# Down-block sums and left-operand sums on GpSimd, operand blocks in two steps, and a last product in two column halves

## The chip, the cores and the metric

The kernel runs on one core of a Trainium2 chip. The metric is device microseconds of one execution, the median of several runs. The engines are TensorE (PE in the profile; PEld is its weight load), VectorE (DVE), ScalarE (ACT), GpSimd (POOL) and SyncE (SP), which here issues the transfers.

## The reference

One encoder layer is applied to two groups of rows that share the weights: 1024 new frames and 32 frames of a running stream. The kernel keeps them side by side as 1056 columns of one activation `x` (1024 features in 8 tiles of 128 partitions). Cut to what matters here:

```python
x = x + 0.5 * swiglu(rms_norm(x, ffn1_norm), ffn1_w_gate, ffn1_w_up, ffn1_w_down)
...   # conv group, HGRN2 group, output projection, attention over 256 memory tokens
x = x + 0.5 * swiglu(rms_norm(x, ffn2_norm), ffn2_w_gate, ffn2_w_up, ffn2_w_down)
y = rms_norm(x, final_norm)      # rms over the 1024 features of a frame

def swiglu(x, w_gate, w_up, w_down):            # 1024 -> 2816 -> 1024
    return (jax.nn.silu(x @ w_gate) * (x @ w_up)) @ w_down
```

Everything is float32. The change touches the two feed-forward networks (FFN1, FFN2) and the final norm.

## The kernel before

**Products.** Each float32 operand is split into a high half (rounded to the type `fp32r`, made by ScalarE) and a low half (operand minus high half, made by VectorE). A product takes three passes on TensorE: high by high, weight high by activation low, weight low by activation high. So a block of weights is usable once ScalarE and then VectorE have worked on it (`Blocks.block`, L498 and L499, for the up products; `DownBlocks.make`, L588 and L589, for the down products).

**Seven products for eight.** Most of each FFN goes by a scheme of Strassen's kind: operands are cut in 2 x 2 quarters, and sums of quarters are multiplied, in the order `a11, s2, s3, a12, s1, a22, s4` for up and `a11, s1, s2, s3, a22, s4, a12` for down (`DORDER`). The sums of the activations ("left operands") for the up products are made in place in `x` by `build` (L784 through its `add`, 16 for each FFN), after the normed rows were made; the sums of the up weights by `Blocks.make` (L513). In the down phase the sums of weights are made by `DownBlocks.make`, one for each of 6 blocks of four of the seven kinds (L576 s1, L579 s2, L582 s3, L584 a22), and the sums of the hidden activations were made in the up phase and lie in memory, from where `Hidden.load` (L543) brings them and `Hidden.split` splits them (L296, L297).

**Down phase.** `down_phase` runs over 7 kinds, 4 row tiles `mp` of 128 output features and 11 k steps. A k step is six matmuls of 264 columns (L876, L877, L880, two column halves `u` each), 48 of them to a block of 8 k steps. At the first k step of a block it asks for the third block after it (`blocks.ready(b + 3)`). After the 11 k steps `take` adds the product to the residual `x` (L828, and L839/L842 for a running sum `u`), whose halves `load_x` (L824) brings back from memory during the first three kinds. Raw weights come in 512 KB tiles (`wraw`, 4 buffers; high and low halves have 3 buffers each).

**What sets the order.** The FFNs are written under a manual schedule: on the engines of `START` (VectorE, TensorE, ScalarE) instructions run in the order in which the code writes them. Generators are interleaved with the products: `tick()` after each k step advances background jobs, each by its rate (`bg(job, 1.0)` is one yield a tick), and `ready(n)` advances a block generator until n blocks are made. One yield of `Blocks`, `DownBlocks` or `build` is one block or one sum.

**End of the program.** In FFN2's down phase `last2` is called for each finished half row tile of `x`: ScalarE squares it, VectorE adds the squares to `r_t`, and ScalarE scales it by the final norm's gain (L1834). When the second column half is complete, `first_tokens` (0.2 yields a tick) turns and writes token tiles 5 to 8. For the first half, `last_tokens` runs for each pair of row tiles, `(4,5)`, `(6,7)`, `(0,1)`, `(2,3)`: it waits five yields, then turns the columns of token tiles 0 to 4 with transposes on TensorE into `pxf` and `pxs` (L1887), and ScalarE copies them to `y`. The last pair comes with no wait and after the last matmul: sums over features by matmuls with a column of ones (`col_norm`, L1850), a reciprocal root in ten small steps on VectorE (`col_root` L334, `rsqrt`), scaling of `y` in three parts (L1895, L1896, L1897) and five transfers (L1898).

## Time and profile before

| | |
|---|---|
| time, median of 3 runs | 2235.58 us (2233.88 to 2236.37) |
| profiled execution, its own time | 2238.53 us |
| its span | 2236.8 us |
| TensorE busy | 2188.3 us, 98% |
| VectorE busy | 1534.8 us, 69% |
| ScalarE busy | 854.2 us, 38% |
| GpSimd busy | 3.5 us, 20 instructions |
| transfers | 262.56 MB, mean 117 GB/s |

The profile is of one execution. A row of the groups reads: engine, tile written and tiles read, count, then busy time and mean length of one, then the idle time of the engine just ahead of them and who ended it. A row of single instructions begins with its start and length in microseconds; what stands in square brackets at its end is the engine's idle time ahead of it and who ended it. A window row gives, for each engine, busy time and count of instructions, then the granted TensorE clock as a share of full speed, the transfer engines' busy share and GB/s.

### The profile page before, as it was taken

The page shows a single profiled execution, that of the slowest core. Times are in us where ns is not written, and L with a number is a line of the kernel's source. Part 1 is how long each engine was busy: PE and PEld are TensorE (multiplying, and loading weights), DVE is VectorE, ACT ScalarE, POOL GpSimd, SP SyncE. Part 2 cuts the span into 40 slices and gives each one's busy share as a digit, 9 for nine tenths or more (in the row PEclk, how much of TensorE's full clock was granted, in tenths as well). Part 3 has the DMA queues.
Part 4 walks back from the last instruction along what each step waited for, and adds up shares of the span by engine and source line. Part 5 has one row for each costly group of instructions (what it writes and reads, how often), then busy time and mean ns, then how long its engine had stood idle before and what let it go on. Part 6 is the DMA issues. An engine that isn't in the chain of part 4 may idle for free. (4 is left out here: it accounts for less than half of the span.)

```text
span 2236.8 us, 39733 instructions
## 1 busy us (share of the span) xinstructions
PE 2188.3 (98%) x16381; PEld 2136.8 (96%) x16381; DVE 1534.8 (69%) x2502; ACT 854.2 (38%) x1550; POOL 3.5 (0%) x20
## 2 busy tenths in 40 slices
PE   8999999999999999999999999999999999999996
PEld 7999999999999899999889999999999999999896
DVE  6976666676777868898643665588866666667763
ACT  6342322333345512455651432352422322343353
POOL 0000000000000000000000000000000000000000
PEclk9999999999999999999999999999999999999998
DMA  6233233249876721111121211121333233298661
GB/s 212 73 110 125 78 98 116 84 136 310 244 225 185 225 79 50 30 42 38 35 95 54 62 52 53 43 107 48 106 99 116 84 97 119 75 297 256 194 181 64
DMA packets 312407, 262.56 MB, mean 117 GB/s; under 512 B 12580, under 2 KB 251912, under 8 KB 312226
## 3 DMA queue, kind: packets, MB, share of 16 engines
q1 hardware_dynamic: 312226, 260.02, 37.6%
q8 instruction: 129, 2.11, 0.4%
q14 instruction: 52, 0.43, 0.1%
HBM read 196.20 MB, written 63.77 MB: 116 GB/s over the span
## 5 line engine op out<-in xcount | busy, mean ns | idle before, releaser
L690 PE MATMUL ps<-A,vhi 128*128 128x264 f32 x1216 | 321.0, 284 | 2.1 <-DVE t L749 2.1
L691 PE MATMUL ps<-A,vhi 128*128 128x264 f32 x1216 | 320.6, 284 | 0.0
L694 PE MATMUL ps<-A,vlo 128*128 128x264 f32 x1216 | 247.4, 285 | 0.0
L691 PE MATMUL pa<-a,vhi 128*128 128x264 f32 x912 | 241.6, 285 | 0.0
L690 PE MATMUL pa<-a,vhi 128*128 128x264 f32 x912 | 241.4, 285 | 0.0
L876 PE MATMUL pdn<-A,vhi 128*128 128x264 f32 x880 | 234.5, 287 | 4.7 <-ACT vhi L588 4.7
L877 PE MATMUL pdn<-A,vhi 128*128 128x264 f32 x880 | 233.2, 286 | 0.0
L690 PEld LDWEIGHTS ps<-A,vhi 128*128 128x128 f32 x1216 | 229.1, 188 | 2.5 <-DVE t L749 2.3
L691 PEld LDWEIGHTS ps<-A,vhi 128*128 128x128 f32 x1216 | 228.7, 188 | 0.0
L694 PEld LDWEIGHTS ps<-A,vlo 128*128 128x128 f32 x1216 | 188.3, 188 | 0.0
L694 PE MATMUL pa<-a,vlo 128*128 128x264 f32 x912 | 185.0, 284 | 0.0
L880 PE MATMUL pdn<-A,vlo 128*128 128x264 f32 x880 | 181.1, 287 | 1.6 <-DVE vlo L589 1.5
L876 PEld LDWEIGHTS pdn<-A,vhi 128*128 128x128 f32 x880 | 167.4, 190 | 5.5 <-ACT vhi L588 5.5
L690 PEld LDWEIGHTS pa<-a,vhi 128*128 128x128 f32 x912 | 171.9, 189 | 0.0
L206 ACT ACTIVATE whi<-wraw 128x1024 fp32r<-128x1024 f32 x74 | 78.1, 1058 | 245.5 <-PE pwo L215 51.3
L691 PEld LDWEIGHTS pa<-a,vhi 128*128 128x128 f32 x912 | 171.3, 188 | 0.0
L877 PEld LDWEIGHTS pdn<-A,vhi 128*128 128x128 f32 x880 | 166.8, 190 | 0.0
L1224 DVE SCALAR_TENSOR_TENSOR ycv<-uy,dwc,ycv 128x1086 f32<-128x1086 f32 x120 | 157.0, 1342 | 0.6
L694 PEld LDWEIGHTS pa<-a,vlo 128*128 128x128 f32 x912 | 141.3, 188 | 0.0
L499 DVE TENSOR_TENSOR vlo<-b_s,vhi 128x512 fp32r<-128x512 f32 x114 | 78.7, 691 | 91.0 <-ACT vhi L498 91.0
L880 PEld LDWEIGHTS pdn<-A,vlo 128*128 128x128 f32 x880 | 137.5, 190 | 3.4 <-DVE vlo L589 3.2
L498 ACT ACTIVATE vhi<-b_s 128x512 fp32r<-128x512 f32 x114 | 71.2, 625 | 175.8 <-DVE b_s L513 174.8
(385 smaller groups left out, 5302.8 us busy)
## 6 DMA issues: line engine op xcount, KB each, us to landing
hd<-t SPq DMA_DIRECT2D x154, 264.0 KB
hraw<-hd SPq DMA_DIRECT2D x154, 264.0 KB
wraw<-in_ffn_w_up SPq DMA_DIRECT2D x44, 512.0 KB
wraw<-in_ffn_w_gate SPq DMA_DIRECT2D x42, 512.0 KB
wraw<-in_ffn_w_down SPq DMA_DIRECT2D x36, 512.0 KB
wraw<-in_w_in SPq DMA_DIRECT2D x24, 512.0 KB
xd<-x SPq DMA_DIRECT2D x32, 264.0 KB
x<-xd SPq DMA_DIRECT2D x32, 264.0 KB
```

Of the source, the lines that this page charges most:

```text
L206: act.activation(hi, t[:, :w], AF.Copy)
L498: act.activation(hi, src, AF.Copy)
L499: dve.tensor_tensor(lo, src, f32(hi), ALU.subtract)
L690: pe.matmul(o, hi[:, k, :], l[:, 0, q], start=start and k == 0, stop=False, **kw)
L691: pe.matmul(o, hi[:, k, :], l[:, 1, q], start=False, stop=False, **kw)
L694: pe.matmul(o, lo[:, k, :], l[:, 0, q], start=False, stop=k == KH - 1, **kw)
L876: pe.matmul(o, wh, l[:, 0, q], start=k == 0, stop=False)
L877: pe.matmul(o, wh, l[:, 1, q], start=False, stop=False)
L880: pe.matmul(o, wl, l[:, 0, q], start=False, stop=k == NJ - 1)
L1224: dve.scalar_tensor_tensor(ycv[:, ct, :], src, w, ycv[:, ct, :], ALU.mult, ALU.add)
```

## The change

1. *Blocks in two steps.* `Blocks` and `DownBlocks` yield between the high half on ScalarE and the low half on VectorE, and count high halves in `begun`. `begin(n)` asks for n high halves, `ready(n)` for n whole blocks. In a product the next block's high half is asked for ahead of its first k step and the low half at its third; the same in the down phase for the third block ahead.
2. *Sums on GpSimd.* The 24 sums of down blocks of each FFN, and the 16 sums of left operands of each, are issued on GpSimd instead of VectorE. GpSimd becomes one of the engines that run in written order (`START`). The yields of `build` are arranged anew: the first four sums interleave with the splits of a22, the next eight take two yields each, and the last four follow at once.
3. *The last product in two column halves.* For a12, `mp` 3 of FFN2 `down_phase` keeps its 11 operand triples, runs all k steps for columns 0 to 263, adds to the residual, and then for columns 264 to 527. `last_part(m, u)` closes each half: the sum of `r_t` over features, multiplied by 1/D in the column `inv`, and apart from it the sum of this tile's own squares, meet in `col_root` (`part`). Token tiles 0 and 1 are turned, scaled on ScalarE and written out six k steps into the second half; tiles 2, 3 and 4 after it, partly on VectorE.
4. *Turned columns later.* `last_tokens` waits nine yields instead of five, and its groups are `(4,5)`, `(6,7)`, `(0,1)`, `(2)`; row tile 3 belongs to `last_part`.

The diff, without `START`, the counters' initial values and a signature, and with the old text of `last_tokens` cut:

```diff
@@ -328,10 +328,13 @@
 
-    def col_root(pc, m, n):
-
-        cv = const.tile([P, 3, 9], F32, tag="cv", name="cv", bufs=1)
-        dve.tensor_scalar(cv[:, 0, :m], pc[:, :m], 1.0 / n, EPS, ALU.mult, ALU.add)
+    def col_root(pc, m, n, part=None):
+
+        cv = const.tile([P, 3, 9], F32, tag="cv", name="cv", bufs=2)
+        if part is not None:
+            dve.tensor_tensor(cv[:, 0, :m], part[:, :m], pc[:, :m], ALU.add)
+        else:
+            dve.tensor_scalar(cv[:, 0, :m], pc[:, :m], 1.0 / n, EPS, ALU.mult, ALU.add)
...
@@ -496,8 +499,11 @@
             act.activation(hi, src, AF.Copy)
+            self.begun += 1
+            yield
             dve.tensor_tensor(lo, src, f32(hi), ALU.subtract)
             self.made.append((hi.rearrange("p (k n) -> p k n", k=KH), lo.rearrange("p (k n) -> p k n", k=KH)))
+            yield
...
@@ -520,8 +526,11 @@
                         diff("s3", b22, b12)
-                    self.block(b[nm])
-                    yield
+                    yield from self.block(b[nm])
+
+        def begin(self, n):
+            while self.begun < n and next(self.gen, 0) is None:
+                pass
...
@@ -573,22 +582,28 @@
                         keep[u] = own(self.lp, 6 + u, [P, 2 * TH], F32, "keep")[:, :n * P]
-                        dve.tensor_tensor(keep[u], raw[0], raw[1], ALU.subtract)
+                        pool.tensor_tensor(keep[u], raw[0], raw[1], ALU.subtract)
                         src = keep[u]
                     elif nm == "s2":
-                        dve.tensor_tensor(keep[u], raw[0], keep[u], ALU.subtract)
+                        pool.tensor_tensor(keep[u], raw[0], keep[u], ALU.subtract)
                         src = keep[u]
                     elif nm == "s3":
-                        dve.tensor_tensor(src, raw[0], raw[1], ALU.subtract)
+                        pool.tensor_tensor(src, raw[0], raw[1], ALU.subtract)
                     elif nm == "a22":
-                        dve.tensor_tensor(keep[u], keep[u], raw[0], ALU.subtract)
+                        pool.tensor_tensor(keep[u], keep[u], raw[0], ALU.subtract)
                         src = keep[u]
                     hi = wpool.tile([P, 1024], F32R, tag="whi", name="vhi")[:, :n * P]
                     lo = wpool.tile([P, 1024], F32R, tag="wlo", name="vlo")[:, :n * P]
                     act.activation(hi, src, AF.Copy)
+                    self.begun += 1
+                    yield
                     dve.tensor_tensor(lo, src, f32(hi), ALU.subtract)
                     self.made.append((hi.rearrange("p (k n) -> p k n", k=n), lo.rearrange("p (k n) -> p k n", k=n)))
                     yield
+
+        def begin(self, n):
+            while self.begun < n and next(self.gen, 0) is None:
+                pass
...
@@ -679,10 +694,13 @@
             blocks = self.blocks
-            blocks.ready(v + 1 + AHEAD)
+            blocks.ready(v + AHEAD)
+            blocks.begin(v + 1 + AHEAD)
             hi, lo = blocks.made[v]
             blocks.made[v] = None
             for k in range(KH):
+                if k == 2:
+                    blocks.ready(v + 1 + AHEAD)
...
@@ -781,7 +799,7 @@
         def add(dst, p_, q, op):
-            dve.tensor_tensor(dst, p_, q, op)
+            pool.tensor_tensor(dst, p_, q, op)
...
@@ -795,17 +813,18 @@
             yield
-        yield from puts(*[("a22", k, x[:, KH + k, h1]) for k in range(KH)])
-        for k in range(KH):
+        for k, _ in enumerate(puts(*[("a22", k, x[:, KH + k, h1]) for k in range(KH)])):
             add(x[:, KH + k, h1], x[:, KH + k, h1], x[:, k, h1], ALU.add)
             yield
         for k in range(KH):
             add(x[:, k, h1], x[:, k, h0], x[:, k, h1], ALU.subtract)
             yield
+            yield
             add(x[:, k, h0], x[:, KH + k, h1], x[:, k, h0], ALU.subtract)
             yield
+            yield
+        for k in range(KH):
             add(x[:, KH + k, h0], x[:, KH + k, h0], x[:, k, h0], ALU.subtract)
-            yield
...
@@ -855,14 +875,19 @@
                  "s2": lambda mp: ((mp, 1),)}
+        parts = []
         for pi, nm in enumerate(DORDER):
             for mp in range(NM2):
                 pt = two("pdn")
                 for k in range(NJ):
                     i = mp * NJ + k
                     if i % KT == 0:
-                        blocks.ready(pi * NU + i // KT + 3)
-                        hi, lo = blocks.made[pi * NU + i // KT]
+                        b = pi * NU + i // KT
+                        blocks.ready(b + 1)
+                        blocks.begin(b + 3)
+                        hi, lo = blocks.made[b]
+                    elif i % KT == 2:
+                        blocks.ready(b + 3)
...
@@ -871,6 +896,9 @@
                     wh, wl = hi[:, i % KT, :], lo[:, i % KT, :]
+                    if last_part and pi == len(DORDER) - 1 and mp == NM2 - 1:
+                        parts.append((wh, wl, l))
+                        continue
...
@@ -879,7 +907,22 @@
                     tick()
+                if parts:
+                    break
                 take(nm, mp, pt[:, :, :QB])
+        jobs = []
+        for u in range(2 if parts else 0):
+            o, q = pt[:, u, :QB], slice(u * QB, (u + 1) * QB)
+            for k, (wh, wl, l) in enumerate(parts):
+                pe.matmul(o, wh, l[:, 0, q], start=k == 0, stop=False)
+                pe.matmul(o, wh, l[:, 1, q], start=False, stop=False)
+                pe.matmul(o, wl, l[:, 0, q], start=False, stop=k == NJ - 1)
+                tick()
+            xs = x[:, mp, q]
+            dve.scalar_tensor_tensor(xs, o, 0.5, xs, ALU.mult, ALU.add)
+            jobs.append(bg(last_part(mp, u), start=True))
+        for j in jobs:
+            drain(j)
...
@@ -1829,16 +1872,61 @@
 
-        sum_sq(x3p, x, m, sl=half(hf), w=TH, first=not sums[hf])
         sums[hf] += 1
-        act.activation(x[:, m, half(hf)], x[:, m, half(hf)], AF.Copy, scale=gcol("final_norm", m))
+        xs = x[:, m, half(hf)]
+        sum_sq(x3p, x, m, sl=half(hf), w=TH, first=sums[hf] == 1)
+        act.activation(xs, xs, AF.Copy, scale=gcol("final_norm", m))
         if hf == 1 and sums[1] == KT:
             bg(first_tokens(), 0.2)
-        if hf == 0 and m % 2:
-            end = sums[0] == KT
-            job = bg(last_tokens(m - 1, end), 1.0)
-            if end:
-                drain(job)
+        if hf == 0 and m != NM2 - 1 and (m % 2 or m == NM2 - 2):
+            bg(last_tokens((m - 1, m) if m % 2 else (m,)), 1.0)
+
+    def last_part(m, u):
+
+        q = slice(u * QB, (u + 1) * QB)
+        tts = (2, 3, 4) if u else (0, 1)
+        if u == 0:
+            Y["sq"] = x3p.tile([P, 5 * P], F32, tag="sq5", name="sq5", bufs=1)
+            Y["mean"] = const.tile([P, 2, 4], F32, name="mean")
+            Y["inv"] = const.tile([P, 1], F32, name="inv")
+            dve.memset(Y["inv"], 1.0 / D)
+            dve.memset(Y["sq"][:, TH:], 0.0)
+            Y["xg"] = own(lp, 11, [P, 2 * TH], F32, "xg")
+            dve.tensor_copy(Y["xg"][:, TH:5 * P], x[:, m, TH:5 * P])
+        sq, xg = Y["sq"], Y["xg"]
+        xs = x[:, m, q]
+        pc = bank("pc")
+        for j, tt in enumerate(tts):
+            pe.matmul(pc[:, j:j + 1], r_t[:, at_tok(tt)], Y["inv"], start=True, stop=True)
+        if u:
+            dve.tensor_tensor(sq[:, q], xs, xs, ALU.mult)
+        else:
+            act.activation(sq[:, q], xs, AF.Square)
+        mean = Y["mean"][:, u]
+        dve.tensor_scalar(mean[:, :len(tts)], pc[:, :len(tts)], EPS, None, ALU.add)
+        dve.tensor_scalar(xg[:, q], xs, gcol("final_norm", m), None, ALU.mult)
+        yield
+        if not u:
+            for _ in range(5):
+                yield
+        for j, tt in enumerate(tts):
+            pe.matmul(pc[:, 4 + j:5 + j], sq[:, at_tok(tt)], Y["inv"], start=True, stop=True)
+        pt = two("pxf")
+        px = [pt[:, j // 2, j % 2 * P:j % 2 * P + P] for j in range(len(tts))]
+        for j, tt in enumerate(tts):
+            pe.transpose(px[j], xg[:, at_tok(tt)], ident)
+        cs = col_root(pc[:, 4:], len(tts), D, mean)
+        c0, c1 = m * P, (m + 1) * P
+        for j, tt in enumerate(tts):
+            y = y_tile(tt)
+            act.activation(y[:, c1:], y[:, c1:], AF.Copy, scale=cs[j])
+            if u:
+                dve.tensor_scalar(y[:, :c0], y[:, :c0], cs[j], None, ALU.mult)
+                dve.tensor_scalar(y[:, c0:c1], px[j], cs[j], None, ALU.mult)
+            else:
+                act.activation(y[:, :c0], y[:, :c0], AF.Copy, scale=cs[j])
+                act.activation(y[:, c0:c1], px[j], AF.Copy, scale=cs[j])
+            nc.sync.dma_start(out=y_p[0, tt * P:(tt + 1) * P, :], in_=y)
 
...
@@ -1872,34 +1960,22 @@
 
-    def last_tokens(m0, end):
-
-        if not end:
-            for _ in range(5):
-                yield
...
+    def last_tokens(ms):
+
+        for _ in range(9):
+            yield
+        pt, ps = two("pxf"), bank("pxs")
+        c0, c1 = ms[0] * P, (ms[-1] + 1) * P
+        px = [pt[:, tt // 2, tt % 2 * 256:tt % 2 * 256 + c1 - c0] for tt in range(4)] + [ps[:, :c1 - c0]]
         for tt in range(5):
...
+            for j, m in enumerate(ms):
+                pe.transpose(px[tt][:, j * P:(j + 1) * P], x[:, m, at_tok(tt)], ident)
         for tt in range(5):
...
+            act.activation(y_tile(tt)[:, c0:c1], px[tt], AF.Copy)
         yield
```

How it moves instructions, at three places. First VectorE in FFN2's down phase, where the a22 blocks are made beside the residual adds of s3 (`keep` holds a sum of weight quarters, `vhi` and `vlo` are high and low half of a block, `A` and `hraw` hidden activations, `pdn` is the product). Before:

```order
L842 TENSOR_TENSOR u_21040<-u_21040,pdn 128x528
L828 SCALAR_TENSOR_TENSOR x_21034<-u_21040,x_21034 128x528 x2
L314 TENSOR_TENSOR r_t<-r_t,sq 128x528
L584 TENSOR_TENSOR keep<-keep,wraw_22434 128x1024
L589 TENSOR_TENSOR vlo<-keep,vhi 128x1024
L297 TENSOR_TENSOR A<-hraw,A 128x528 x2
L584 TENSOR_TENSOR keep<-keep,wraw_22506 128x1024
L589 TENSOR_TENSOR vlo<-keep,vhi 128x1024
L828 SCALAR_TENSOR_TENSOR x_21034<-pdn,x_21034 128x528
L314 TENSOR_TENSOR r_t<-r_t,sq 128x528
```

And now:

```order
L862 TENSOR_TENSOR u_21040<-u_21040,pdn 128x528
L848 SCALAR_TENSOR_TENSOR x_21034<-u_21040,x_21034 128x528 x2
L314 TENSOR_TENSOR r_t<-r_t,sq 128x528
L600 TENSOR_TENSOR vlo<-keep,vhi 128x1024
L297 TENSOR_TENSOR A<-hraw,A 128x528 x2
L600 TENSOR_TENSOR vlo<-keep,vhi 128x1024
L848 SCALAR_TENSOR_TENSOR x_21034<-pdn,x_21034 128x528
L314 TENSOR_TENSOR r_t<-r_t,sq 128x528
```

The sums into `keep` are gone from VectorE; they stand on GpSimd (L593), in the same order among themselves.

Second, SyncE in FFN1's down phase, where the s2 blocks' raw tiles are fetched (`wraw62` to `wraw66`; a tile can come in two pieces), `hraw` are hidden activations and `x_5700` residual halves. Before:

```order
L174 DMA wraw62_6277<-in_ffn1_w_down 128x8x128
L174 DMA wraw63_6279<-in_ffn1_w_down 128x3x128
L174 DMA wraw63_6279<-in_ffn1_w_down 128x5x128
L543 DMA hraw_6238<-hd_81 128x528
L824 DMA x_5700<-xd_82 128x528 x2
L543 DMA hraw_6269<-hd_81 128x528
L174 DMA wraw64_6345<-in_ffn1_w_down 128x6x128
```

And now:

```order
L174 DMA wraw62_6277<-in_ffn1_w_down 128x8x128
L174 DMA wraw63_6279<-in_ffn1_w_down 128x3x128
L552 DMA hraw_6238<-hd_81 128x528
L174 DMA wraw63_6279<-in_ffn1_w_down 128x5x128
L174 DMA wraw64_6345<-in_ffn1_w_down 128x6x128
L174 DMA wraw64_6345<-in_ffn1_w_down 128x2x128
L844 DMA x_5700<-xd_82 128x528
L552 DMA hraw_6269<-hd_81 128x528
```

The residual half now stands behind both pieces of `wraw64`, which were behind it.

Third, TensorE at the end of the program. Before, all of the turning and the sums stand behind the last matmul of the product:

```order
L876 MATMUL pdn<-A,vhi 128x264
L877 MATMUL pdn<-A,vhi 128x264
L880 MATMUL pdn<-A,vlo 128x264 x2
L1887 MATMUL pxf<-ident,x_21034 128x128 x8
L1887 MATMUL pxs<-ident,x_21034 128x128 x2
L1850 MATMUL pc<-ones,r_t 128x1 x5
```

Now, from within the second column half on:

```order
L917 MATMUL pdn<-A,vhi 128x264
L918 MATMUL pdn<-A,vhi 128x264
L919 MATMUL pdn<-A,vlo 128x264
L1913 MATMUL pc<-inv,sq_23702 128x1 x2
L1917 MATMUL pxf<-ident,xg 128x128 x2
L917 MATMUL pdn<-A,vhi 128x264
```

and behind the last matmul:

```order
L917 MATMUL pdn<-A,vhi 128x264
L918 MATMUL pdn<-A,vhi 128x264
L919 MATMUL pdn<-A,vlo 128x264
L1900 MATMUL pc<-inv,r_t 128x1 x3
L1913 MATMUL pc<-inv,sq_23702 128x1 x3
L1917 MATMUL pxf<-ident,xg 128x128 x3
```

Of the turning of the last row tile and its sums, two token tiles stand inside the second half and three behind it.

More of the change, by code (lines that the diff above doesn't have):

```diff
@@ L62 @@
 ROOT = 4
-START = {mybir.EngineType.DVE, mybir.EngineType.PE, mybir.EngineType.Activation}
+START = {mybir.EngineType.DVE, mybir.EngineType.PE, mybir.EngineType.Activation, mybir.EngineType.Pool}
 ORDERED = {mybir.EngineType.DVE, mybir.EngineType.PE}
@@ L488, in __init__ @@
         def __init__(self, up, tp):
-            self.gen, self.tp, self.made = self.make(up), tp, []
+            self.gen, self.tp, self.made, self.begun = self.make(up), tp, [], 0
         def block(self, src):
@@ L560, in __init__ @@
         def __init__(self, down, lp):
-            self.gen, self.lp, self.made = self.make(down), lp, []
+            self.gen, self.lp, self.made, self.begun = self.make(down), lp, [], 0
         def make(self, down):
@@ L817, in build, with down_phase @@
             yield from puts(*[(nm, k, x[:, k0 + k, h]) for k in range(KH)])
-    def down_phase(hid, blocks, x, up_, last):
+    def down_phase(hid, blocks, x, up_, last, last_part=None):
         U = [up_.tile([P, 2, QB], F32, name=f"u{mp}") for mp in range(NM2)]
@@ L1873, in first_tokens @@
                 nc.sync.dma_start(out=y_s[0], in_=y[P - NS:, :])
-    def last_tokens(m0, end):
-        if not end:
-            for _ in range(5):
-                yield
-        pt = two("pxf")
-        ps = bank("pxs")
-        px = {}
-        ms = slice(m0 * P, (m0 + 2) * P)
-        for tt in range(5):
-            px[tt] = pt[:, tt // 2, tt % 2 * 256:tt % 2 * 256 + 256] if tt < 4 else ps[:, :256]
-            for i in range(2):
-                pe.transpose(px[tt][:, i * P:(i + 1) * P], x[:, m0 + i, at_tok(tt)], ident)
-        if end:
-            cs = col_norm(range(5))
-        for tt in range(5):
-            y = y_tile(tt)
-            if not end:
-                act.activation(y[:, ms], px[tt], AF.Copy)
-                continue
-            act.activation(y[:, ms.stop:], y[:, ms.stop:], AF.Copy, scale=cs[tt])
-            dve.tensor_scalar(y[:, :ms.start], y[:, :ms.start], cs[tt], None, ALU.mult)
-            dve.tensor_scalar(y[:, ms], px[tt], cs[tt], None, ALU.mult)
-            nc.sync.dma_start(out=y_p[0, tt * P:(tt + 1) * P, :], in_=y)
+    def last_tokens(ms):
[4 more added lines that the diff above has]
+        px = [pt[:, tt // 2, tt % 2 * 256:tt % 2 * 256 + c1 - c0] for tt in range(4)] + [ps[:, :c1 - c0]]
+        for tt in range(5):
+            for j, m in enumerate(ms):
+                pe.transpose(px[tt][:, j * P:(j + 1) * P], x[:, m, at_tok(tt)], ident)
+        for tt in range(5):
+            act.activation(y_tile(tt)[:, c0:c1], px[tt], AF.Copy)
         yield
     with tc.manual_schedule(engines=START):
-        down_phase(H["hid"], H["down"], x, x3p, last2)
+        down_phase(H["hid"], H["down"], x, x3p, last2, last_part)
     xs1.close()
```

## The prediction

> **What bounds the kernel now.** I read the page first, then windows of equal length for the stretches in which TensorE is not full, then TensorE's waits, and last the rows of the engines that it waits for.
>
> ```profile
> span 2236.8 us, 39733 instructions
> PE 2188.3 (98%) x16381; PEld 2136.8 (96%) x16381; DVE 1534.8 (69%) x2502; ACT 854.2 (38%) x1550; POOL 3.5 (0%) x20
> ```
>
> TensorE is busy for 98% of the span, and the change takes no matmul of the products away. All it can win is TensorE's idle time, 48.5 us, and what comes of it. Where that lies, the windows say (stretch and length, then busy time and count of PE, PEld, DVE, ACT, POOL, then PEclk, DMA share, GB/s):
>
> ```profile
> 600.00:650.00 50.00, 46.23 (x353) 44.57 (x352) 37.77 (x47) 17.31 (x27) 0.00 (x0) 0.97 0.74 217
> ...
> 1650.00:1700.00 50.00, 50.00 (x412) 50.00 (x411) 32.19 (x50) 13.84 (x25) 0.00 (x0) 1.00 0.35 107
> ...
> 2110.00:2115.00 5.00, 3.73 (x17) 3.51 (x18) 3.78 (x5) 1.65 (x3) 0.00 (x0) 0.66 0.54 162
> ```
>
> In the up products a window is full: 412 matmuls in 50 us, 0.121 us each. In the first down phase 3.8 us are missing, and the granted clock of 0.97 is another 1.5 us (0.03 of 50). In the second down phase a dip of the clock to 0.66 over 5 us costs 1.7 us. So a stall is paid twice. TensorE's waits (who, for whom: us in all, times, longest):
>
> ```profile
> PE pdn L876 <- ACT vhi L588: 6.4, 6, 2.0
> PE pxf L1887 <- ACT x L1834: 6.0, 3, 3.5
> PE pdn L880 <- DVE vlo L589: 2.5, 6, 0.5
> PE ps L690 <- DVE t L749: 2.1, 1, 2.1
> ```
>
> Down blocks cost 8.9 us (3.8 in the first down phase, so 5.1 in the second), the turned columns at the end 6.0, one up product 2.1. Why the blocks are late, three queues show just ahead of the stalls:
>
> ```profile
> DVE vlo L589 <- ACT vhi L588: 70.1, 63, 5.1
> ```
>
> ```profile
> 2084.14 0.65 ACT L309 ACTIVATE r_t<-x 128x528 f32<-128x528 f32 x1 [3.27 <-DVE x L828]
> 2084.82 0.74 ACT L1834 ACTIVATE x<-x,vecs 128x528 f32<-128x528 f32 x1
> 2085.46 1.16 ACT L296 ACTIVATE a<-hraw 128x528 fp32r<-128x528 f32 x2
> 2088.67 1.06 ACT L588 ACTIVATE vhi<-wraw 128x1024 fp32r<-128x1024 f32 x1 [2.04 <-issue]
> ```
>
> ```profile
> 2086.12 1.33 DVE L297 TENSOR_TENSOR a<-hraw,a 128x528 fp32r<-128x528 f32 x2 [2.02 <-ACT a L296]
> 2087.36 1.22 DVE L582 TENSOR_TENSOR wraw<-wraw,wraw 128x1024 f32<-128x1024 f32 x1
> 2089.76 1.23 DVE L589 TENSOR_TENSOR vlo<-wraw,vhi 128x1024 fp32r<-128x1024 f32 x1 [1.18 <-ACT vhi L588]
> ```
>
> VectorE makes the sum of a block, waits 1.2 us for ScalarE's high half, makes the low half; ScalarE in turn waits 3.27 us for a residual add that stands behind VectorE's last low half. Each round is longer than the 48 matmuls of a block (5.8 us), and the lookahead runs out.
>
> **The change part by part.** *Sums of down blocks on GpSimd, blocks in two steps.* Off VectorE go 24 sums per down phase, and the wait of 1.2 us in front of a low half, since the high half is now asked for two k steps (1.45 us) earlier.
>
> ```profile
> L582 DVE TENSOR_TENSOR wraw<-wraw,wraw x12: 683/1217/1219, 591.4 to 2096.2; 128x1024 f32<-128x1024 f32 x10, 128x512 f32<-128x512 f32 x2
> ```
>
> ```profile
> masks.py:199 POOL TENSOR_SCALAR_AFFINE_SELECT ident<-ident 128x128 f32<-128x128 f32 x1 | 0.3, 292 | 0.1
> ...
> L1191 POOL MEMSET r_t<- 128x6 f32 x1 | 0.1, 103 | 0.0
> ```
>
> VectorE's sum is 1.22 us. GpSimd has no two-operand row. Its one-operand row gives (292 - 103)/128 = 1.48 ns an element, so 1.6 us for 1024; if each operand is read in turn, 3.1 us. I take the middle, 2.35 us, an estimate from these two rows. The Trainium skill, GPSIMD Engine Reference, "3.1 Elementwise", has 4497 ns for an add of 2048 floats, 2.25 us for half of it as an estimate, with VectorE at 2293 ns, which fits the 1.22 us here; by it the sum below stays within a microsecond, and the page advises against the move.
>
> What hides the longer sum: it no longer stands in VectorE's queue. Its operands are there early, for only the first kind of sum ever waited for a transfer (L576, below), and the lookahead is two blocks, 11.7 us, against 2.35 + 1.06 + 1.23 = 4.6 us for sum, high and low half. Without that cover each block would be 1.1 us later than now. A raw tile also comes free 1.1 us later, and the transfers queued behind on SyncE with it. On ScalarE the high half now waits for GpSimd, and left operands, squares and scalings stand behind it, as they stood behind VectorE's sum. On SyncE loads of residual halves fall behind loads of raw tiles (the order rows in the change show it). VectorE already waits for them twice:
>
> ```profile
> DVE x L828 <- DMA x<-xd: 14.2, 2, 7.8
> ```
>
> Both waits fall into the first kind of product, where the lead is largest, and stop no TensorE now; I cost the later place at nothing, and at up to 3 us a phase if that lead is gone.
>
> ```profile
> L576 DVE TENSOR_TENSOR keep<-wraw,wraw x12: 681/1220/1226, 523.2 to 2026.6; 128x1024 f32<-128x1024 f32 x10, 128x512 f32<-128x512 f32 x2
> its engine sat idle before it (us, times) until:
>   DMA wraw<-in_ffn_w_down: 6.8, 6
> ```
>
> At stake are 3.8 + 1.5 = 5.3 us in the first down phase and 5.1 + 1.7 = 6.8 in the second. Bounds: all of it, or as much lost if the two engines hinder each other. I take 3.5 and 4.5, two thirds, since GpSimd is slower and the first phase has the smaller lead.
>
> *Sums of left operands on GpSimd.* 32 sums of 528 columns leave VectorE, 16 for each FFN.
>
> ```profile
> L784 DVE TENSOR_TENSOR x<-x 128x528 f32<-128x528 f32 x32 | 21.5, 704 | 0.5
> ```
>
> ```profile
> 1536.00:1566.00 30.00, 29.64 (x244) 29.43 (x243) 28.30 (x42) 7.85 (x12) 0.00 (x0) 1.00 0.24 72
> ```
>
> VectorE is busy 28.3 of 30 us there, and 11.3 us of that are these sums. It is this backlog from which TensorE's 2.1 us wait for t L749 comes. GpSimd needs 0.9 to 1.7 us for each, 1.3 in the middle, 20 us in all, and the last four feed only the product that comes last. What hides them are the plain products still running. I take 1.5 of the 2.1 us (bounds 0 and 2.3); the first FFN has no such stall, so nothing there.
>
> *Turned columns four ticks later.*
>
> ```profile
> 2180.73 0.69 ACT L1868 ACTIVATE y<-pxf,rr 128x512 f32<-128x512 f32 x1 [3.92 <-DMA out<-y]
> ...
> 2185.56 0.74 ACT L1834 ACTIVATE x<-x,vecs 128x528 f32<-128x528 f32 x1
> ```
>
> ```profile
> 2186.35 1.48 PE pxf L1887 x7
> ...
> 2220.85 1.76 PE pxf L1887 x7
> ```
>
> ```profile
> 2185.00:2190.00 5.00, 3.61 (x17) 3.21 (x18) 1.93 (x2) 2.79 (x4) 0.00 (x0) 0.67 0.42 151
> ```
>
> ScalarE waits 3.92 us for an output transfer, so the scaled columns come late, and TensorE stands 3.5 us in front of the turn at 2186.35. Nine yields for five are four k steps of six matmuls, 2.9 us of product work put ahead of it. That leaves 0.6 us, too little, I think, for the dip of the clock at 2185 to 2190 (0.33 of 5 us, 1.65). Together 2.9 + 1.65 + 0.2 for a smaller such stall: 4.7 us (bounds 2.9 and 5.6).
>
> *The end.* Before, after the last matmul at 2218.6:
>
> ```profile
> 2218.65 0.71 DVE L828 SCALAR_TENSOR_TENSOR x<-pdn,x 128x528 f32<-128x528 f32 x1 [5.91 <-PE pdn L880]
> ...
> 2225.00 0.16 DVE L334 TENSOR_SCALAR cv<-pc 128x5 f32<-128x5 f32 x1 [4.23 <-PE pc L1850]
> ...
> 2227.19 0.35 DVE L1896 TENSOR_SCALAR y<-y,cv 128x256 f32<-128x256 f32 x1
> ```
>
> ```profile
> 2222.83 2.13 PE L1850 MATMUL pc<-ones,r_t 128*128 128x1 f32 x10
> ```
>
> ```profile
> 2228.00 4.12 SPq L1898 DMA_DIRECT2D out<-y  x5
> ```
>
> ```profile
> 2231.00:2231.50 0.50, 0.00 (x0) 0.00 (x0) 0.00 (x0) 0.00 (x0) 0.00 (x0) 0.50 1.01 393
> ```
>
> First issue 9.4 us after the matmuls, end 18.2 us after them. From the first issue it is the transfer rate that counts: five tiles of 524 KB at 393 GB/s are 6.7 us, and 2.1 us of the 8.8 stand around them. Now two tiles go out during the second part of the last product, and three after it: 2.1 + 4.0 = 6.1 us. Ahead of them stand the 264-wide add (0.48, by the row below), a square (half of 0.70, I take 0.42), three column sums (two passes each; 0.21 a pass at half clock, 0.11 at full: 0.65), the root from 2225.00 to 2227.19 (2.2, unchanged), first rows to first issue 0.8, hand-overs 0.2: 4.75 us. TensorE has seven transposes and four sums more ahead of its end, 0.8 + 0.85 = 1.65 us. The root of the first two tiles ends about 0.3 us after the matmuls on the same queue. So 18.2 - 4.75 - 6.1 - 1.65 - 0.3 = 5.4 us; I take 5.2 (bounds 3.5, with sums at half clock and late tiles, and 6.3).
>
> ```profile
> L1021 DVE SCALAR_TENSOR_TENSOR A<-pxt,vecs,A 128x264 fp32r<-128x264 f32 x18 | 8.7, 481 | 0.0
> ```
>
> **Sum.** 3.5 + 4.5 + 1.5 + 4.7 + 5.2 = 19.4 us. The profiled execution took 2238.5 us (span 2236.8 and 1.7 around it), 2.9 above the median of 2235.6. 2238.5 - 19.4 = 2219.1, and against the median 2216.
>
> **The rivals.** *The two engines take turns.* VectorE's work on down blocks is nearly all two operands in SBUF.
>
> ```profile
> 2065.00:2085.00 20.00, 20.00 (x167) 20.00 (x166) 15.23 (x19) 5.90 (x9) 0.00 (x0) 1.00 0.86 251
> ```
>
> It is busy 15.2 of 20 us there, 4.45 per block of 5.83 us, 3.2 without the sum. If GpSimd's sum shuts VectorE out for its whole length, 3.2 + 2.35 = 5.6 us: it just fits, but nothing is regained, stalls stay as they are, and the opening gains nothing either. Then only the 9.9 us of the end remain: 2226. For it: every VectorE low half reads two tiles. Against: the wait of 1.2 us per block goes in any case. The same time comes out if late transfers, not queues, are what makes blocks late; against that speaks that two kinds of sum of four never waited for one. The Trainium skill, SBUF — State Buffer, "Who interferes with whom", states this lock, exclusive and for the whole instruction, for VectorE with two SBUF inputs against a GpSimd read; no run here shows it yet.
>
> *Slower.* The same turn-taking with the dear price. VectorE's other waits are 0.3 us a block (4.8 idle in 20, less three waits of 1.2 for high halves). 3.2 + 0.3 + p exceeds 5.83 from p = 2.3 on; at 3.1 each of 24 blocks is 0.8 late, 19 us a phase, less 3 of lead, 32 in both, for the 12.1 that stalls and clock cost now. Plus 20, less the 9.9 of the end: 2246. For it: the two-reads bound. Against: part of VectorE's work reads PSUM, and GpSimd runs ahead of need.
>
> **How the numbers follow.** Forecast, 2208 to 2222: 0.62. Taking turns, 2222 to 2231: 0.23. Slower, 2240 and more: 0.08. The rest, 0.07, is a new wait that eats the gain and lands within 0.2% (4.5 us, about what can be told from no change here). The lower bound is all terms at their best, 26 us: 2209; the upper one holds the turn-taking case with some microseconds more. Faster 0.85, same 0.07, slower 0.08.
>
> **What would show it.** Right: no pdn wait for vhi or vlo worth a microsecond, PEclk 1.00 in both down phases, VectorE's wait for vhi near nothing, GpSimd sums of some 2.3 us, last matmul to end of span about 11 us. Wrong: VectorE rows of 128x1024 well over 1.22 us beside a GpSimd row (turns), GpSimd sums of 3 us and more, ScalarE idle before vhi because of GpSimd, or a pxf wait still of 2 us.

## The result and the profile after

The changed kernel is slower: 2253.27 us median (2251.99 to 2256.15, 4 runs), against 2235.97 us (2233.88 to 2240.53, 4 runs) before; ratio 1.0076, 95% interval 1.0058 to 1.0095. The forecast was 2216. The profiled execution took 2253.0 us, its span follows.

The page after, totals:

```profile
span 2251.3 us, 39788 instructions
PE 2189.3 (97%) x16391; PEld 2141.2 (95%) x16391; DVE 1541.0 (68%) x2437; ACT 856.0 (38%) x1558; POOL 176.6 (8%) x100
```

GpSimd took over 173 us of sums, and VectorE is not relieved: it does 65 instructions fewer and is busy 6 us longer. The two windows below (the columns are those of the prediction) show it. In the first down phase, which begins 2 us later than before, TensorE had 46.23 us of work in 50 and now has 43.04; VectorE was busy 37.77 us with 47 instructions, and is busy 41.75 us with 38, beside ten sums on GpSimd. The second window lies in the worst stall.

```profile
600.00:650.00 50.00, 43.04 (x341) 42.83 (x340) 41.75 (x38) 18.00 (x26) 22.86 (x10) 0.93 0.77 233
...
2125.00:2130.00 5.00, 0.00 (x0) 0.00 (x0) 4.29 (x3) 1.22 (x2) 4.83 (x3) 0.50 0.60 174
```

In those 5 us VectorE works on three instructions, which are 0.7 us each before, and is busy 4.29 us with them; TensorE does nothing. TensorE's waits after (us in all, times, longest):

```profile
PE pdn L908 <- DVE vlo L600: 25.1, 7, 10.1
...
PE ps L708 <- DVE t L767: 6.2, 2, 3.2
...
PE ps L708 <- DVE t L657: 1.7, 1, 1.7
...
PE pdn L904 <- ACT vhi L597: 0.9, 1, 0.9
```

Waits for turned columns are gone from the list; down blocks cost 26.0 us where they cost 8.9, the openings 7.9 where they cost 2.1. The table gives the length of each stage in the two profiles, from the start of its first matmul to that of the next stage. All the other tables of this section are made in the same way.

| stage (us) | before | after | difference |
|---|---|---|---|
| start to FFN1's first fast product | 109.5 | 107.1 | -2.4 |
| FFN1 fast up products | 390.0 | 394.4 | +4.5 |
| FFN1 down phase | 233.9 | 242.4 | +8.4 |
| from there to FFN2's first fast product | 845.9 | 844.3 | -1.6 |
| FFN2 fast up products | 391.7 | 397.1 | +5.4 |
| FFN2 down phase up to its last product | 239.4 | 244.1 | +4.7 |
| last product to end of span | 26.4 | 21.8 | -4.5 |

The two stages that the change doesn't touch move by -2.4 and -1.6 with the dips of the clock (mean granted clock 0.95 before and 0.97 after in the first, 0.99 and 1.00 in the second); the four with GpSimd's sums lose 23.0 us together, the end gains 4.5.

**Where VectorE's time went.** Groups of VectorE by form, first before, then after. The first row reads one operand from PSUM (`pdn`) and one from SBUF, the second both from SBUF:

```profile
L828 DVE SCALAR_TENSOR_TENSOR x<-pdn,x 128x528 f32<-128x528 f32 x48 | 33.0, 700 | 29.1 <-PE pdn L880 14.8 <-DMA x<-xd 14.2
L828 DVE SCALAR_TENSOR_TENSOR x<-u,x 128x528 f32<-128x528 f32 x24 | 16.3, 706 | 0.5
```

```profile
L848 DVE SCALAR_TENSOR_TENSOR x<-pdn,x 128x528 f32<-128x528 f32 x47 | 32.3, 700 | 31.1 <-PE pdn L908 16.9 <-ACT u L853 7.6 <-DMA x<-xd 6.3
L848 DVE SCALAR_TENSOR_TENSOR x<-u,x 128x528 f32<-128x528 f32 x24 | 31.7, 1348 | 0.5
```

The same instruction with a PSUM operand keeps its 700 ns; with both operands in SBUF its mean goes from 706 to 1348 ns. The single rows of the worst stall (start and length) say how:

```profile
2119.59 2.46 POOL L593 TENSOR_TENSOR keep<-keep,wraw 128x1024 f32<-128x1024 f32 x1 [1.91 <-DMA wraw<-in_ffn_w_down]
2123.05 6.79 POOL L593 TENSOR_TENSOR keep<-keep,wraw 128x1024 f32<-128x1024 f32 x3 [1.00 <-DMA wraw<-in_ffn_w_down]
...
2119.82 2.80 DVE L297 TENSOR_TENSOR A<-hraw,A 128x528 fp32r<-128x528 f32 x1
2122.54 0.69 DVE L862 TENSOR_TENSOR u<-u,pdn 128x528 f32<-128x528 f32 x1
2123.26 5.45 DVE L848 SCALAR_TENSOR_TENSOR x<-u,x 128x528 f32<-128x528 f32 x2
...
2130.32 1.21 DVE L600 TENSOR_TENSOR vlo<-keep,vhi 128x1024 fp32r<-128x1024 f32 x1
...
2131.59 0.81 PE L908 MATMUL pdn<-a,vlo 128*128 128x264 f32 x2 [10.05 <-DVE vlo L600]
```

VectorE's row from 2119.82 ends at 2122.62, and GpSimd's beside it at 2122.05: 0.57 us of own work behind it. The row with `pdn` takes its 0.69. Then GpSimd does three sums one behind the other, because raw tiles had come in together, and each of VectorE's two adds lasts 2.7 us. The wait for the other engine lies inside VectorE's rows and not in the idle time ahead of them. GpSimd's price is read from the first down phase, where it ran while VectorE stood idle:

```profile
540.09 2.39 POOL L585 TENSOR_TENSOR keep<-wraw,wraw 128x1024 f32<-128x1024 f32 x1 [3.95 <-DMA wraw<-in_ffn_w_down]
```

### The profile page after: what moved, and what is told of

It is laid out like the page before. It is cut to its first block, busy times and chain, and to the rows that moved or that the text cites. A ratio compares the mean times of both kernels' runs of the same rounds, so it can differ in the third digit from the quotient of the medians.

```text
span 2251.3 us, 39788 instructions
## 1 busy us (share of the span) xinstructions
PE 2189.3 (97%) x16391; PEld 2141.2 (95%) x16391; DVE 1541.0 (68%) x2437; ACT 856.0 (38%) x1558; POOL 176.6 (8%) x100
## 5 line engine op out<-in xcount | busy, mean ns | idle before, releaser
L708 PEld LDWEIGHTS ps<-A,vhi 128*128 128x128 f32 x1216 | 231.1, 190 | 8.5 <-DVE t L767 6.6
L709 PEld LDWEIGHTS ps<-A,vhi 128*128 128x128 f32 x1216 | 230.7, 190 | 0.0
L904 PE MATMUL pdn<-A,vhi 128*128 128x264 f32 x866 | 229.8, 286 | 0.1
L905 PE MATMUL pdn<-A,vhi 128*128 128x264 f32 x866 | 228.5, 285 | 0.0
L908 PE MATMUL pdn<-A,vlo 128*128 128x264 f32 x866 | 176.4, 285 | 1.1 <-DVE vlo L600 1.1
L904 PEld LDWEIGHTS pdn<-A,vhi 128*128 128x128 f32 x866 | 164.1, 189 | 0.3 <-ACT vhi L597 0.3
L905 PEld LDWEIGHTS pdn<-A,vhi 128*128 128x128 f32 x866 | 163.5, 189 | 0.0
```

What stands on the lines that cost most here:

```text
L708: pe.matmul(o, hi[:, k, :], l[:, 0, q], start=start and k == 0, stop=False, **kw)
L709: pe.matmul(o, hi[:, k, :], l[:, 1, q], start=False, stop=False, **kw)
L904: pe.matmul(o, wh, l[:, 0, q], start=k == 0, stop=False)
L905: pe.matmul(o, wh, l[:, 1, q], start=False, stop=False)
L908: pe.matmul(o, wl, l[:, 0, q], start=False, stop=k == NJ - 1)
```

## The experiments

The theory (A): while a GpSimd instruction reads two SBUF operands, VectorE can't start one that reads two. The rivals: late transfers by the new order of issues (B), and a chain that is longer only because GpSimd is slow (C). The three sets of runs were each compared with the kernel before on the same chip, whose median there was 2233.94, 2236.27 and 2235.29 us.

### Which part costs what

**All sums back on VectorE.** In the changed kernel `pool.tensor_tensor` becomes `dve.tensor_tensor` in `DownBlocks.make` and in `build`.

```diff
-                        pool.tensor_tensor(keep[u], raw[0], raw[1], ALU.subtract)
+                        dve.tensor_tensor(keep[u], raw[0], raw[1], ALU.subtract)
...
         def add(dst, p_, q, op):
-            pool.tensor_tensor(dst, p_, q, op)
+            dve.tensor_tensor(dst, p_, q, op)
```

> The change with both kinds of sums put back on VectorE; blocks in two steps and the new end stay. Theory A (GpSimd's sums shut VectorE out of its own two-operand work while they run): the new stalls go, TensorE's idle time falls from 11.6 and 14.5 us in the two down phases to at most the 3.8 and 5.2 of before; 2213 to 2226 us, 2221 if the two steps regain half of that. Theory B (the two steps order raw loads ahead of hidden and residual loads, and the transfers come late): the stalls stay where they are, and only the openings recover, some 8 us: 2245. Theory C (a GpSimd sum is only longer, 2.45 us for 1.22, without shutting anyone out): as A, 2213 to 2226.

Measured: 2221.84 us (2218.41 to 2224.25), ratio to before 0.9946 (0.9928 to 0.9964).

**Only the sums of left operands back** (the second piece of that diff).

> The change with only the 32 sums of left operands back on VectorE; down-block sums stay on GpSimd. A, B and C alike: the openings recover, where TensorE waited 2.94 and 3.24 us for a VectorE row and the clock dipped after each for some 1.7: 2253 - 8 = 2245 us (2242 to 2248). If the openings are as slow as in the changed kernel, the two steps of the up blocks are to blame and not these sums: 2253.

Measured: 2247.06 us, ratio 1.0065 (1.0043 to 1.0086).

**Only the sums of down blocks back** (the first piece, at all four sums).

> The change with only the 48 sums of down blocks back on VectorE; sums of left operands stay on GpSimd. A and C: 7.8 and 9.3 us of TensorE's idle time and some 3 us of clock go: 2253 - 20 = 2233 us (2228 to 2237). B (late transfers by the new order): the stalls of 3.0, 7.0 and 10.1 us stay: 2250 or more.

Measured: 2226.97 us, ratio 0.9970 (0.9956 to 0.9984).

| stage (us) | before | after | all on VectorE | left sums back | down sums back |
|---|---|---|---|---|---|
| FFN1 up | 390.0 | 394.4 | 390.9 | 390.9 | 394.5 |
| FFN1 down | 233.9 | 242.4 | 231.6 | 242.7 | 231.7 |
| FFN2 up | 391.7 | 397.1 | 394.2 | 394.3 | 396.0 |
| FFN2 down to last product | 239.4 | 244.1 | 231.8 | 243.4 | 230.7 |
| last product to end | 26.4 | 21.8 | 21.8 | 21.8 | 22.1 |

The two costs stand side by side: sums of down blocks on GpSimd cost 25 us (2247.06 - 2221.84), those of left operands 5 (2226.97 - 2221.84), each in its own stages. B falls: with the sums on VectorE and the order of issues that the two steps give, the stalls of 3.0, 7.0 and 10.1 us are gone. GpSimd's waits for transfers I take to follow from blocks that freed their buffers late; no run tests that by itself. The run with the down sums back lies a microsecond below its expected range.

**Only the new end.** Last product in halves, nine yields; everything else as before.

```diff
-                        blocks.ready(b + 1)
-                        blocks.begin(b + 3)
+                        blocks.ready(b + 3)
                         hi, lo = blocks.made[b]
-                    elif i % KT == 2:
-                        blocks.ready(b + 3)
```

(against the changed kernel; the same in `Blocks`, and all sums and `build` as before)

> Only the end of the change: the last product in two column halves and the turned columns nine yields later; blocks in one step, all sums on VectorE, as before. In the two profiles the stretch from the second output tile row of FFN2's last products to the end of the span took 84.6 us before and 74.0 in the changed kernel, 10.6 less, on either theory of the rest. Expected: 2236 - 10.6 = 2225.4 us (2222 to 2228). If the end gained only because it was reached later, with transfers already drained, it is under 5 us: 2231 or more.

Measured: 2230.38 us (10 runs, 2228.4 to 2235.04), ratio 0.9987 (0.9978 to 0.9997); 3.6 us, not 10.6. The last product to the end takes 21.8 us for 26.4, as in the changed kernel. The FFN2 down phase ahead of it takes 241.2 for 239.4: TensorE's wait for turned columns was not removed, it stands at another turn, that of the finished rows (`first_tokens`). TensorE and ScalarE there:

```profile
2180.67 0.98 PE L1961 MATMUL pxf<-ident,x 128*128 128x128 f32 x7 [0.48 <-ACT x L1867]
2182.19 0.44 PE L1961 MATMUL pxs<-ident,x 128*128 128x128 f32 x2 [0.54 <-ACT y L1945]
...
2185.68 1.11 PE L1944 MATMUL pxf<-ident,x 128*128 128x128 f32 x4 [2.32 <-ACT y L1945]
```

```profile
2184.94 0.69 ACT L1945 ACTIVATE y<-pxf,rr 128x512 f32<-128x512 f32 x1 [2.80 <-DMA out<-y]
```

The cause is the one that stood at L1868 before, ScalarE's wait for an output transfer; four yields later it only meets another turn.

### Whether it is a lock

**Extra sums that nobody reads.** The kernel before, with 24 more sums on GpSimd in FFN2's down phase on a tile of their own.

```diff
                     self.made.append((hi.rearrange("p (k n) -> p k n", k=n), lo.rearrange("p (k n) -> p k n", k=n)))
+                    if nm in ("s1", "s2", "s3", "a22") and self.extra is not None:
+                        d = self.extra
+                        pool.tensor_copy(d[:, :1], f32(lo)[:, :1])
+                        pool.tensor_tensor(d, d, d, ALU.subtract)
```

> The kernel before, and beside it in FFN2's down phase 24 more sums of 128x1024 on GpSimd, on a tile of its own that nothing reads; each starts when a block's low half is made. Nothing waits for them. Theory A (a GpSimd sum shuts VectorE out of work on two SBUF operands while it runs): VectorE rows beside them grow by up to 2.3 us (1.22 to 3.5, 0.70 to 3.0); 4.45 us of VectorE work a block and 2.3 are 6.8 against 5.83 of matmuls, 24 blocks late by 0.9 less some lead: plus 10 to 20 us, 2244 to 2254. Theory C (the sums are only slower and the chain of a block longer): VectorE rows stay at 1.22 and 0.70 us and the time at 2234, within 3.

Measured: 2263.45 us (2261.62 to 2265.43), ratio 1.0130 (1.0114 to 1.0145): 27 us, more than the 10 to 20 expected, for work that nothing waits for. (The copy of one column lets each sum start when a low half is made.)

**The same with one operand** (`pool.tensor_scalar(d, d, 0.5, None, ALU.mult)` for the subtract).

> As the run with extra sums, but the extra GpSimd work reads one operand (128x1024 scaled by a constant). If GpSimd shuts VectorE out for the length of any of its instructions, VectorE rows grow by its length, some 1.5 us, and the time by 0 to 8 us. If the shutting out needs two operands on GpSimd, rows stay at 1.22 and 0.70 us, and the time at 2234, within 3.

Measured: 2245.39 us, ratio 1.0047 (1.0030 to 1.0065): 9 us. The groups of GpSimd and VectorE, two operands and then one:

```profile
L594 POOL TENSOR_TENSOR extra<-extra 128x1024 f32<-128x1024 f32 x24 | 48.3, 2012 | 2.1 <-POOL extra L593 0.2
...
L835 DVE SCALAR_TENSOR_TENSOR x<-u,x 128x528 f32<-128x528 f32 x12 | 19.2, 1623 | 0.3
...
L579 DVE TENSOR_TENSOR keep<-wraw,keep 128x1024 f32<-128x1024 f32 x5 | 10.2, 2040 | 0.0
```

```profile
L594 POOL TENSOR_SCALAR extra<-extra 128x1024 f32<-128x1024 f32 x24 | 69.3, 2890 | 2.2 <-POOL extra L593 0.2
...
L835 DVE SCALAR_TENSOR_TENSOR x<-u,x 128x528 f32<-128x528 f32 x12 | 12.3, 1053 | 0.3
...
L579 DVE TENSOR_TENSOR keep<-wraw,keep 128x1024 f32<-128x1024 f32 x5 | 7.8, 1551 | 0.0
```

C falls as the whole answer: no block's chain holds these sums, and VectorE's rows still grow, from 706 to 1623 ns and from some 1217 to 2040. Over all its forms in the stage, mean growth times count is about 31 us with two operands and 12 with one, near the 27 and 9 us that the runs cost. With one operand GpSimd's row is longer (2890 ns for 2012) and VectorE loses less. Pairs of single rows, GpSimd and then VectorE, say why, first with two operands:

```profile
2046.46 2.25 POOL L594 TENSOR_TENSOR extra<-extra 128x1024 f32<-128x1024 f32 x1
```

```profile
2046.88 2.92 DVE L579 TENSOR_TENSOR keep<-wraw,keep 128x1024 f32<-128x1024 f32 x1
```

and with one:

```profile
2046.77 2.77 POOL L594 TENSOR_SCALAR extra<-extra 128x1024 f32<-128x1024 f32 x1 [0.22 <-POOL extra L593]
```

```profile
2046.88 1.48 DVE L835 SCALAR_TENSOR_TENSOR x<-u,x 128x528 f32<-128x528 f32 x1
```

Beside two operands VectorE's sum, 1.22 us alone, ends 1.09 us behind GpSimd's row. With one, its add, issued 0.11 us behind a GpSimd row of 2.77, grows by 0.77 and not by 2.7: about the first 0.9 us of the one-operand instruction hold it up, the rest does not. The other adds of that form agree. In each run eight of them begin 0.11 to 0.53 us behind such a GpSimd row, and wherever they begin, they end 2.45 to 2.46 us behind its start with two operands (its row is 1.89 there) and 1.60 us behind it with one. That is a hold up to a fixed point and not a slower pace. My two expectations (a whole row, or nothing) were both wrong for it.

**Sums in four pieces.** The changed kernel, each down sum on GpSimd in pieces of 256 columns.

```diff
+    def pieces(o_, a_, b_, op):
+        for c in range(0, o_.shape[-1], 256):
+            pool.tensor_tensor(o_[:, c:c + 256], a_[:, c:c + 256], b_[:, c:c + 256], op)
```

> The changed kernel with each sum of a down block on GpSimd in four pieces of 256 columns. If GpSimd shuts VectorE out by the instruction, VectorE gets its turn between pieces: its longest rows shrink from 2.9 to some 1.9 us for 128x528, though the sum of the lengthening stays if the shared time stays; the time 2240 to 2253. If what counts is the traffic and not whose instruction is running, rows lengthen as in the changed kernel and the time is 2253 or, by four fixed starts a sum, more.

Measured: 2252.83 us, ratio 1.0080 (1.0063 to 1.0095), as the changed kernel. The rows follow the first expectation, GpSimd and then VectorE:

```profile
2123.84 2.55 POOL L568 TENSOR_TENSOR keep<-keep,wraw 128x256 f32<-128x256 f32 x3 [0.64 <-DMA wraw<-in_ffn_w_down]
```

```profile
2123.26 1.87 DVE L852 SCALAR_TENSOR_TENSOR x<-u,x 128x528 f32<-128x528 f32 x2
```

```profile
L852 DVE SCALAR_TENSOR_TENSOR x<-u,x 128x528 f32<-128x528 f32 x24 | 22.7, 974 | 0.5
```

Two adds that took 5.45 us beside whole sums take 1.87 here, and their mean falls from 1348 to 974 ns: VectorE waits for a piece, not for a sum, so the lock goes by the instruction. Nothing is won by it, since GpSimd now waits more: its 44 pieces of each of three kinds (s2, s3, a22) take 133 us, where their sums took 90, and the blocks come no earlier. Shorter turns move the wait between the engines and do not shorten it.

### What the rest of the change is worth

**Only the blocks in two steps** (the kernel before with `begun`, `begin` and the two yields; sums on VectorE).

> The kernel before with only the blocks in two steps; sums on VectorE, old end. With the new end the two steps and the new order of the left operands' sums were worth 8.6 us (2230.4 to 2221.8), nearly all of it behind the start of FFN2's down phase. If that belongs to the block chain alone, it shows here too: 2234 - 8 = 2226. If it belongs to the turned columns, which ScalarE reaches earlier and which only the later turn makes use of, little is left: 2230 to 2234, with TensorE waits for turned columns still there.

Measured: 2226.19 us (9 runs, 2220.53 to 2234.02), ratio 0.9950 (0.9935 to 0.9966). The FFN2 down phase to its last product takes 231.4 us, as in the runs with the new end (231.8, 230.7), and TensorE's wait of 3.5 us for turned columns is gone with five yields. Waits for down blocks are 8.3 us in all there, for 8.9 before: the two steps hardly touch what they were costed for, and cure the turned columns. Why they cure it is not tested by itself. The output transfer that ScalarE waits for ahead of that turn took 4.97 us from its issue to ScalarE's next row before, with three loads of raw tiles issued ahead of it; here it takes 3.00, with three such loads issued behind it, and ScalarE's wait is 1.97 us for 3.92. So the new order on SyncE is as good a candidate as the earlier high half. The runs scatter (the profiled execution is the slowest of the nine), so how much of the 10 us is the clock stays open; the stage alone is 8.

**All sums on VectorE, left sums at their old yields** (`build` as before).

> All sums on VectorE, two steps, new end, and the sums of left operands at the yields of the kernel before. With the new yields TensorE waited 0.84 and 3.20 us in the two openings, with the old ones 0 and 2.1: 2222 - 2 = 2220 us. If the wait in the second opening stays at 3.2, the two steps of the up blocks cause it.

Measured: 2226.02 us, ratio 0.9961 (0.9947 to 0.9976). TensorE's waits in the openings stay at 0.84 and 3.0 us; the order of `build` is not their cause.

**Only the down blocks in two steps**, up blocks in one, all sums on VectorE, `build` as before, new end.

```diff
             act.activation(hi, src, AF.Copy)
-            self.begun += 1
-            yield
             dve.tensor_tensor(lo, src, f32(hi), ALU.subtract)
...
-            blocks.ready(v + AHEAD)
-            blocks.begin(v + 1 + AHEAD)
+            blocks.ready(v + 1 + AHEAD)
```

> Only the down blocks in two steps, the up blocks in one as before; all sums on VectorE and at their old yields; new end. If the two steps of the up blocks cause the new waits in the openings (0.84 and 3.0 us, 0 and 2.1 before), these go: 2 us of idle time and the clock that follows, 12 to 14 us less than the kernel before in all, 2221 where that has 2235. If not, as the run with all sums on VectorE at their old yields, 10 less.

Measured: 2218.24 us (2214.38 to 2224.38, 6 runs), ratio 0.9921 (0.9905 to 0.9936): 17 us less than before, some 35 less than the changed kernel, the best of all. Its waits and a window:

```profile
PE pdn L902 <- DVE vlo L598: 6.9, 5, 2.6
...
DVE vlo L598 <- ACT vhi L595: 56.6, 49, 3.8
...
PE ps L703 <- DVE t L762: 2.1, 1, 2.1
...
PE pdn L898 <- ACT vhi L595: 0.8, 1, 0.8
```

```profile
600.00:650.00 50.00, 47.63 (x390) 47.20 (x389) 37.43 (x49) 19.29 (x28) 0.00 (x0) 1.00 0.73 218
```

VectorE's wait for the high half, 70.1 us in 63 times before, is still 56.6 in 49. The openings are as before (FFN1's wait is gone, FFN2's is 2.1), so the two steps of the up blocks cost the 0.84 and the 0.9 above 2.1. That is less than the step in time from the run ahead of it (ratio 0.9961 to 0.9921, some 9 us); where the rest comes from stays open. The window of the first down phase has 47.63 us of TensorE where it had 46.23 before and 43.04 in the changed kernel. What is left at the down blocks is 7.7 us, nearly all in front of VectorE's low half.

**The same with five yields** in `last_tokens`.

> The same with the turned columns waiting five yields again instead of nine. In the run of the two steps alone, with five yields, TensorE's wait of 3.5 us for turned columns was gone already. If the two steps had cured it, the time is the same within 1 us and no wait for turned columns over 0.5 us is there. If the later turn is needed beside the new end, a wait of 1 to 3.5 us comes back and some 3 us of time.

Measured: 2219.39 us (2216.01 to 2228.51), ratio 0.9935 (0.9917 to 0.9953), no difference to nine that can be told. No wait for turned columns is in it either, and the stage to the last product is 231.1 us for 231.4. The later turn is worth nothing that can be told once the blocks go in two steps.

## Why the prediction was wrong, step by step

- **Sums of down blocks on GpSimd** (8.0 us of gain): the step that failed. The price was right: 2.35 us estimated, 2.39 measured with nothing beside it. What failed is "it no longer stands in VectorE's queue": it stood there all the same, inside VectorE's rows. The rival in which the two engines take turns was written down, and given too little: 0.23, with 2226 us, and 0.08 in its dear form. That form's "2240 and more" holds the measured time, but by a price of 3.1 us a sum, which was not there. The prediction's own arithmetic spoke against the forecast: 3.2 + 0.3 + p exceeds a block's 5.83 from p = 2.3 on, and the value taken was 2.35; "it just fits" left out the 0.3. With the 2.5 to 2.75 us that the rows show beside VectorE each block is 0.2 to 0.4 late, by estimate some 4 to 10 us a phase before the lead is taken off; against the run with all sums on VectorE, 10.8 are measured in FFN1's (242.4 and 231.6) and 12.3 in FFN2's (244.1 and 231.8). The sum by averages also missed the bursts: raw tiles that come in together make GpSimd do three sums in a row, 6.8 us in which VectorE, for whose queue TensorE waits, got through two adds. "Its operands are there early" did not hold either: GpSimd's s3 sums waited 58.7 us in ten times for raw tiles.
- **Blocks in two steps.** That VectorE's wait of 1.2 us for the high half would go in any case was wrong for the most part: 56.6 of 70.1 us of it stay in the best run, and down-block waits fell only from 8.9 to 7.7 us. What the two steps did win stands mostly at the turned columns.
- **Sums of left operands on GpSimd** (1.5 us of gain): wrong by sign. They cost 5 us. GpSimd's row was forecast at 1.3 us and is 1.31 at its shortest, but 1.78 us in the mean beside VectorE, and VectorE's rows beside it that read two SBUF operands grew (`t<-t` of 128x528 from 706 to 780 ns in the mean of 88). The price of the two steps in the up blocks, some 2 us, had no term at all.
- **Turned columns four ticks later** (4.7 us of gain): wrong cause. The wait did go, but the two steps took it away; the later turn alone moved it to another turn (2.32 us there), and with the two steps it adds nothing.
- **The end** (5.2 us): right in mechanism, 4.5 measured. Two of its sentences did not fit together: two tiles were to go out during the second part of the last product, and their root was to end 0.3 us behind it. The first issue came 1.6 us behind the last matmul (its end is at 2240.1). It cost little, since the three late tiles set the end, and they follow the 264-wide add and square as forecast; the last matmul to the end took 11.1 us, where "about 11" had been named:

```profile
2240.16 0.43 DVE L922 SCALAR_TENSOR_TENSOR x<-pdn,x 128x264 f32<-128x264 f32 x1
2240.63 0.43 DVE L1902 TENSOR_TENSOR sq<-x 128x264 f32<-128x264 f32 x1
```

```profile
2241.73 4.95 SPq L1929 DMA_DIRECT2D out<-y  x5
```

- **The signs named beforehand** were the right ones: VectorE's rows far over their length beside GpSimd's were to show the turns, and do. "GpSimd sums of some 2.3 us" held as well, and by itself proved nothing.

The Trainium skill, SBUF — State Buffer, "Who interferes with whom", was cited in the prediction with this lock; the runs bear it out: exclusive, by the instruction, for VectorE with two SBUF inputs, and not for one with a PSUM input (700 ns before and after). The same page, "SBUF: two separate sides", has the one that starts first hold the pair for the whole instruction; the one-operand row here differs: 0.9 us of 2.77 held VectorE up.

## What to carry to other kernels

Before an elementwise operation moves from VectorE to GpSimd, count what VectorE does meanwhile with both operands in SBUF: that work waits while GpSimd reads two operands, so a sum that takes twice as long there makes VectorE's queue longer and not shorter. Rows of VectorE that grow only beside rows of GpSimd, while rows with a PSUM operand keep their length, are the sign. A wait at the end of a chain of queues is better taken away ahead in that chain than by moving its consumer, which can meet the same wait at the next place (here 2.32 us at the next turn, for 3.5).

## What the runs showed of the hardware beside that

A one-operand GpSimd instruction of 128x1024 took 2.77 us where two operands took 1.89 on the same tile (2.25 where the row had to wait for VectorE's first), and held VectorE up for a third of its length only. Sums in four pieces gave VectorE its turn after each piece of some 0.73 us and left the time of the kernel the same (2252.83 and 2253.27 us).
